# Pair products in quarters of the array, and the last two column tiles in stretches of 304 and 240 tokens, in one layer of a hybrid recurrent decoder

## The chip, the core and the metric

The kernel runs on one core of a Trainium2 chip. A core has a matrix engine (TensorE, here PE; its weight loads are listed apart as PEld), a vector engine (DVE), a scalar engine (ACT), a general engine (POOL), and a queue engine (SP) that issues most of the DMAs. The engines run side by side; each works through its own list of instructions in order and waits on semaphores for the others. The metric is the time of one execution in microseconds (us), lower is better. Before the change the median of three executions is 925.21 us (924.53 to 926.5).

## What is computed

One decoder layer is run for 512 prompt tokens and 8 x 4 sample tokens, which together are the 544 columns of every activation. One input projection feeds three recurrent branches (GLA, mLSTM, HGRN2); their gated sum goes through an output projection and a LayerNorm, then through an MLP and a second LayerNorm. Two of the branches, GLA and HGRN2, are this recurrence, which the kernel evaluates in chunks:

```python
def step(s, blk):
    qc, kc, vc, gc = blk
    b = jnp.cumsum(gc, axis=1)
    o_inter = jnp.einsum("bthk,bhkv->bthv", qc * jnp.exp(b), s)
    rel = jnp.exp(jnp.where(causal, b[:, :, None] - b[:, None, :], -jnp.inf))
    att = jnp.sum(qc[:, :, None] * kc[:, None, :] * rel, axis=-1)
    o_intra = jnp.einsum("btsh,bshv->bthv", att, vc)
...
hid = jnp.square(jax.nn.relu(x @ lp["w_ff_up"]))
x = _layernorm(DN_ALPHA * x + (hid @ lp["w_ff_down"]), lp["ln2_g"], lp["ln2_b"])
```

`att` is a matrix of pair products: entry (t, s), for a query token t and a key token s not after it. The outputs are the layer's result, transposed, and the new recurrent states.

## The kernel before, in words

Activations lie transposed: 128 features on the partitions, 544 tokens along them. A weight matrix comes in tiles of 128 output features (column tiles). For each, `wload` issues a DMA from SP, copies the tile on ACT into a rounded high part `wh` and subtracts on DVE the low part `wl`; `mm` (line 157) then runs three matmuls for each 128 rows of the weight (high x high, high x low, low x high), each on two halves of 272 tokens. These are the matmuls `g` of line 170. `wh` and `wl` have three buffers from the merge stage on, so a tile's copy waits until the PE has finished the tile three loads earlier. The result lies in a pair of PSUM banks, of which there are two pairs.

The two gated recurrences are in `gated` (line 363), first GLA ("gla"), then HGRN2 ("hg"). Tokens come in units u: two of 256 prompt tokens (u = 0, 1), each of C = 2 chunks of R = 128, and the 32 sample tokens (u = 2). `levels(u)` builds the pair products of a unit in a tile `at`: first the diagonal (matmuls `dps`, line 381, then ACT copies of an identity scaled by each head's diagonal, line 388), then the rest by levels m = 64, 32, 16, 8, 4, 2, 1. At a level a block of 2m tokens gives the products of its first m keys with its last m queries. For each level DVE and ACT make the scaled keys `K` (tile ke, line 407) and queries `Q` (tile qe, line 414), the PE multiplies them (`lv`, line 422), and DVE writes the valid entries into `at` under a mask (line 426). Each level's matmul covers all 128 keys of a chunk at once and so also products that no block needs; the mask drops them. ke and qe have two buffers each, used in turn. `chunk(u, c)` then forms the chunk's output `o` from `at` and the state `S` (lines 482, 485), the state update `kvp` (line 490), a norm over each head (`rms_rows`: ACT square, DVE reduce, ACT logarithm and exponential `ss`, DVE product `on`), a transpose `oT` on the PE and its product with the gate. `sample` is the same for u = 2, with matmuls `ox` (line 527) that write 32 PSUM partitions each.

Between these small steps stand background matmuls `g` of column tiles that do not depend on the recurrence. No table sets their order: a scheduler in the framework simulates the program and places each instruction on its engine's list; evacuations and weight copies carry a high priority.

At the end, the last two column tiles of the MLP (features 6 and 7 of 8) are kept back and run by halves of the tokens, so that the second LayerNorm of the first half overlaps the matmuls of the second. `last(i, hf, sl)` runs one tile on one half, `ln_sums` and `ln_end` form mean and inverse deviation (`ne`, `rstd`), and then for each of eight feature tiles DVE adds `ne` (line 1132) and multiplies by `rstd` (line 1136), ACT applies scale and offset (line 1140), and SP stores pairs of tiles (line 1142).

Of the kernel before, what the change touches and what calls it, by code (L numbers as in the profile page):

```python
# [6 lines left out]
F32 = mybir.dt.float32  # L7
# [22 lines left out]
ADDP, MULP, AFFD = (), (), ()  # L30
# [12 lines left out]
def build(tc, I, O):  # L43
    nc = tc.nc
    with ExitStack() as ctx:
# [59 lines left out]
        nc.scalar.dma_start(out=mf_[:, 0:448], in_=I["lmask"])  # L105
        lmask = const.tile([128, 7, 64], I32, name="lmask")
        nc.vector.tensor_copy(lmask.rearrange("p a b -> p (a b)"), mf_[:, 0:448])
        mf2 = wp.tile([128, 1024], F32, tag="raw", name="mf2", bufs=3)
        nc.scalar.dma_start(out=mf2[:, 0:160], in_=I["cmask"])
# [3 lines left out]
        nc.vector.tensor_copy(smask, mf2[:, 128:160])  # L113
        identb = const.tile([128, 128], BF16, name="identb")
# [42 lines left out]
        def mm(ps, units, ah, al, ext=0, halves_=(0, 1), between=None):  # L157


            nk = sum(u[2] for u in units)  # L160
            k = 0
            for u, (h, l, n) in enumerate(units):
                if u and between:
                    between()
                for i in range(n):
                    wh, wl = h[:, i * 128:(i + 1) * 128], l[:, i * 128:(i + 1) * 128]
                    for s, (w, a) in enumerate(((wh, ah), (wh, al), (wl, ah))):
                        for hf in halves_:
                            w_ = HT + (ext if hf else 0)
                            nc.tensor.matmul(  # L170
                                ps[:, hf, 0:w_], w, a(k)[:, hf * HT:hf * HT + w_],
                                start=(k == 0 and s == 0), stop=(k == nk - 1 and s == 2))
                    k += 1
# [189 lines left out]
        def gated(q, k, b, sc, dv, vtok, sname, nt, gate):  # L363
# [5 lines left out]
            def levels(u):  # L369
# [9 lines left out]
                for c in range(C):  # L379
                    for p in range(2):  # L380
                        nc.tensor.matmul(dps[0:R, c * 4 + p * 2:c * 4 + p * 2 + 2], qk[:, p, c * R:(c + 1) * R], headsel,  # L381
                                         start=(c == 0 and p == 0), stop=(c == C - 1 and p == 1))
                dsb = t1.tile([128, 8], F32, tag="dsb", name="dsb")
                nc.vector.tensor_copy(dsb[0:R, 0:4 * C], dps[0:R, 0:4 * C])
                at = kqp.tile([128, 8, 128], F32, tag="at", name="at", bufs=2)
                atv = at[0:R, 0:4 * C, 0:R]
                for j in range(4 * C):
                    nc.scalar.activation(out=at[0:R, j, 0:R], in_=ident[0:R, 0:R], func=AF.Copy, scale=dsb[0:R, j:j + 1])

                for li, m in enumerate(LEVELS):  # L390
                    if 2 * m > B:
                        continue
                    n = L // (2 * m)
                    nr = R // (2 * m)
                    blk = lambda a: a.rearrange("p a (n m) -> p a n m", m=2 * m)
                    K, Q = ke[li % 2], qe[li % 2]
                    bb = blk(bv)
                    ref = bb[:, :, :, m - 1:m].to_broadcast([128, 2, n, m])
                    E = tile2([128, 2, 256], "E")
                    Ev = blk(E[:, :, 0:L])  # L400
                    if m > 1:
                        ref2 = bb[:, :, :, m - 1:m].to_broadcast([128, 2, n, 2 * m])
                        nc.vector.tensor_tensor(out=Ev, in0=bb, in1=ref2, op=ALU.subtract)
                        nc.scalar.activation(out=Ev[:, :, :, 0:m], in_=Ev[:, :, :, 0:m], func=AF.Exp, scale=-sc)
                        nc.scalar.activation(out=Ev[:, :, :, m:2 * m], in_=Ev[:, :, :, m:2 * m], func=AF.Exp, scale=sc)
# [12 lines left out]
                    H = R // 2  # L418
                    for c in range(C):
                        for p in range(2):  # L420
                            o = (c * 2 + p) * 2 * H
                            nc.tensor.matmul(  # L422
                                lv[0:R, o:o + 2 * H].rearrange("p (a b) -> p a b", a=2),
                                Kv[:, p, c * R:(c + 1) * R], Q[:, p, :, c * H:(c + 1) * H],
                                start=(c == 0 and p == 0), stop=(c == C - 1 and p == 1))
                    nc.vector.copy_predicated(
                        atv.rearrange("p h (n m) -> p h n m", m=2 * m)[:, :, :, m:2 * m],
                        lmask[0:R, li, 0:H].rearrange("p (n m) -> p n m", m=m)[:, None].to_broadcast([R, 4 * C, nr, m]),
                        lv[0:R, 0:4 * C * H].rearrange("p (h n m) -> p h n m", h=4 * C, m=m))
                    yield  # L430
                yield
# [412 lines left out]
        def open_kq():  # L844
            st, kqp = pool("kq", 1, "right")
            ke = [kqp.tile([128, 2, 256], F32, name=f"ke{i}") for i in range(2)]
            qe = [kqp.tile([128, 2, 2, 128], F32, name=f"qe{i}") for i in range(2)]
            for t in ke + qe:
                nc.gpsimd.memset(t, 0.0)
            return st, kqp, ke, qe  # L850
# [23 lines left out]
        kqs, kqp, ke, qe = open_kq()  # L874
# [85 lines left out]
        kqs, kqp, ke, qe = open_kq()  # L960
# [52 lines left out]
        def ln_sums(hf, stop=True):  # L1013
            s = slice(hf * HT, (hf + 1) * HT)
            ps = [psr.tile([128, 512], F32, tag="r", name=n) for n in ("m1", "m2")]
            for p, a in zip(ps, (a1, a2)):
                nc.tensor.matmul(p[:, 0:HT], onesn, a[:, s], start=True, stop=stop)  # L1017
            return ps

        def ln_end(hf, sums, more=()):  # L1020
            s = slice(hf * HT, (hf + 1) * HT)
            p1, p2 = sums
            for p, a in zip(sums, more):
                nc.tensor.matmul(p[:, 0:HT], onesn, a, start=False, stop=True)
            e2 = rstd[:, s]
            nc.scalar.activation(out=e2, in_=p1[:, 0:HT], func=AF.Square)
            nc.vector.tensor_tensor(out=e2, in0=p2[:, 0:HT], in1=e2, op=ALU.subtract)
            nc.scalar.activation(out=ne[:, s], in_=p1[:, 0:HT], func=AF.Copy, scale=-1.0)
# [24 lines left out]
        for hf in range(2):  # L1053
            ln_end(hf, ln_sums(hf))
# [55 lines left out]
        def last(i, hf, sl, between=None):  # L1110
            y = x1[:, KD - 2 + i, sl]
            mm(pss[i], units[2 * i:2 * i + 2], hh_, hl_, halves_=(hf,), between=between)
            sq = ftile("sq")
            with tc.high_priority(OFF):
                nc.vector.tensor_tensor(out=y, in0=y, in1=pss[i][:, hf, 0:HT], op=ALU.add)
                nc.scalar.activation(out=sq[:, sl], in_=y, func=AF.Square)
            return y, sq[:, sl]

        for hf in range(2):
            sl = slice(hf * HT, (hf + 1) * HT)  # L1120
# [5 lines left out]
            more = last(1, hf, sl, lambda: ends.append(ln_sums(hf, False)))  # L1126
            with tc.high_priority(OFF):
                ln_end(hf, ends[0], more)
            for m in range(KD):
                y = x1[:, m, sl]  # L1130
                eng = nc.gpsimd if m in ADDP else nc.vector
                eng.tensor_tensor(out=y, in0=y, in1=ne[:, sl], op=ALU.add)
            for m in range(KD):
                y = x1[:, m, sl]
                eng = nc.gpsimd if m in MULP else nc.vector
                eng.tensor_tensor(out=y, in0=y, in1=rstd[:, sl], op=ALU.mult)
                if m in AFFD:
# [14 lines left out]
def _pack(v):  # L1152
# [45 lines left out]
    lmask = np.zeros((128, 7, 64), f)  # L1198
    for i, m in enumerate(LEVELS):
        j = np.arange(64)  # L1200
        lmask[:, i] = ((s[:, None] // (2 * m) == j[None] // m) & (s[:, None] % (2 * m) < m))
# [21 lines left out]
        ident=np.eye(128, dtype=f), lmask=lmask.reshape(128, 448), cmask=np.concatenate([cmask, sm], 1), small=small, lastsel=last,  # L1223
# [42 lines left out]
```

## Time and profile before

| what | value |
|---|---|
| median of three executions | 925.21 us |
| the profiled execution | 923.02 us, of which its span 921.2 us |
| PE busy | 902.4 us |
| DVE busy | 574.3 us |
| ACT busy | 438.3 us |
| POOL busy | 49.6 us |
| GLA recurrence, roughly | 181 to 287 us of the span |
| HGRN2 recurrence, roughly | 312 to 420 us |
| after the last matmul | 911 to 921.2 us |

The span runs from the first to the last recorded instruction. A line such as "L422" is the kernel's line 422. In a timeline a row gives the start, the length of the whole run of like instructions, engine, line, operation, output and inputs, shapes and count; in brackets the engine's idle time before it and what ended it. A float32 matmul of the program shows as two matmuls in the trace, since it is run in two passes; the program's own list, in the section on the change, counts it once.

### The profile page before, as it was taken

To read this page: it belongs to the slowest core of one execution; us is meant where nothing else is said; L and a number is where in the kernel's file an instruction comes from. 1 tells how busy PE (TensorE), PEld (TensorE's weight loads), DVE (VectorE), ACT (ScalarE), POOL (GpSimd) and SP (SyncE) were. 2 spreads that over 40 slices of the span, in tenths; PEclk is the share of its full clock that TensorE was granted. 3 is DMA by queue.
4 is the path that set the end of the run, shared out by engine and by line. 5 is a ranking of instruction groups with operands and counts; after the bars stand their busy time and mean duration, and the time that the engine had idled before them with its cause. 6 is when DMAs were issued, how large, how long until landed. Compare 5 with 4: busy or idle time off the path is not lost.

```text
span 921.2 us, 17477 instructions
## 1 busy us (share of the span) xinstructions
PE 902.4 (98%) x7257; PEld 886.6 (96%) x7257; DVE 574.3 (62%) x1008; ACT 438.3 (48%) x826; POOL 49.6 (5%) x63
## 2 busy tenths in 40 slices
PE   9999999999998999999999999999999999999995
PEld 8998999999998999999999999999999999999994
DVE  5886567788697779785568755554333455444525
ACT  5395323677445875634544455442222345542305
POOL 1301230001001101000000000000000000000000
PEclk9999999999999999999999999999999999999998
DMA  7321242133321113122244222222222222222202
GB/s 267 126 70 69 62 133 83 49 102 89 127 69 41 52 54 98 56 71 86 89 146 142 81 92 92 93 92 75 87 92 92 92 90 74 90 92 92 92 1 98
DMA packets 38335, 82.87 MB, mean 90 GB/s; under 512 B 13156, under 2 KB 19332, under 8 KB 38256
## 3 DMA queue, kind: packets, MB, share of 16 engines
q1 hardware_dynamic: 25664, 73.41, 24.6%
q10 hardware_dynamic: 12528, 8.33, 3.2%
q8 instruction: 57, 0.93, 0.4%
q14 instruction: 22, 0.18, 0.1%
q0 software_dynamic: 64, 0.02, 0.0%
HBM read 76.51 MB, written 5.09 MB: 89 GB/s over the span
## 4 chain that ended last, share of the span: by engine, by line
PE 97%; DVE 2%; ACT 1%; issue 0%; ACTq 0%; DVEq 0%
PE g L170 83%; PE lv L422 3%; PE g L92 3%; PE o L482 1%; PE qkp L701 1%; PE oT L298 0%; PE o L485 0%; PE vt L271 0%; PE kvp L490 0%; PE m L1017 0%; PE na L743 0%; ACT merged L1140 0%; PE wps L64 0%; PE dps L381 0%; PE sp L718 0%; PE kvm L754 0%
## 5 line engine op out<-in xcount | busy, mean ns | idle before, releaser
L154 DVE TENSOR_TENSOR wl<-raw,wh 128x1024 fp32r<-128x1024 f32 (+2 forms) x139 | 154.8, 1113 | 136.9 <-ACT wh L153 136.0
L153 ACT ACTIVATE wh<-raw 128x1024 fp32r<-128x1024 f32 (+2 forms) x139 | 133.3, 959 | 200.9 <-PE g L170 169.3
L170 PE MATMUL g<-xh,wl 128*128 128x272 f32 x752 | 161.1, 291 | 0.0
L170 PE MATMUL g<-xh,wh 128*128 128x272 f32 x752 | 159.8, 291 | 0.3 <-DVE z L863 0.3
L170 PE MATMUL g<-xl,wh 128*128 128x272 f32 x752 | 157.0, 289 | 0.0
L170 PEld LDWEIGHTS g<-xh,wh 128*128 128x128 f32 x752 | 118.7, 189 | 1.8 <-DVE z L863 0.5
L170 PEld LDWEIGHTS g<-xh,wl 128*128 128x128 f32 x752 | 119.0, 188 | 1.1 <-issue 0.2
L170 PEld LDWEIGHTS g<-xl,wh 128*128 128x128 f32 x752 | 118.4, 188 | 0.1
L170 PE MATMUL g<-x1l,wh 128*128 128x272 f32 (+1 forms) x512 | 106.7, 289 | 0.0
L170 PE MATMUL g<-x1h,wh 128*128 128x272 f32 (+1 forms) x512 | 106.4, 289 | 0.0
L170 PE MATMUL g<-x1h,wl 128*128 128x272 f32 (+1 forms) x512 | 106.3, 289 | 0.0
L170 PEld LDWEIGHTS g<-x1l,wh 128*128 128x128 f32 x512 | 81.3, 189 | 0.1
L170 PEld LDWEIGHTS g<-x1h,wh 128*128 128x128 f32 x512 | 81.0, 189 | 0.0
L170 PEld LDWEIGHTS g<-x1h,wl 128*128 128x128 f32 x512 | 80.9, 188 | 0.0
L1070 ACT ACTIVATE relu<-relu,gw 128x544 f32<-128x544 f32 x32 | 24.0, 750 | 78.9 <-DVE relu L1069 78.9
L170 PE MATMUL g<-hidl,wh 128*128 128x272 f32 x280 | 58.2, 289 | 0.0
L170 PE MATMUL g<-hidh,wh 128*128 128x272 f32 x280 | 58.1, 288 | 0.0
L170 PE MATMUL g<-hidh,wl 128*128 128x272 f32 x280 | 58.0, 288 | 0.0
L170 PEld LDWEIGHTS g<-hidl,wh 128*128 128x128 f32 x280 | 44.1, 189 | 0.0
L170 PEld LDWEIGHTS g<-hidh,wh 128*128 128x128 f32 x280 | 44.0, 188 | 0.0
L170 PEld LDWEIGHTS g<-hidh,wl 128*128 128x128 f32 x280 | 44.0, 188 | 0.0
L170 PE MATMUL g<-hdw,wh 128*128 128x272 f32 x168 | 34.8, 289 | 0.0
(399 smaller groups left out, 1633.6 us busy)
## 6 DMA issues: line engine op xcount, KB each, us to landing
raw<-in_wff SPq DMA_DIRECT2D x64, 512.0 KB
raw<-in_win SPq DMA_DIRECT2D x47, 512.0 KB
raw<-in_wout SPq DMA_DIRECT2D x8, 512.0 KB
xr<-in_xT SPq DMA_DIRECT2D x15, 272.0 KB
out_yT<-merged SPq DMA_DIRECT2D x8, 272.0 KB
fw<-in_wfirst ACTq DMA_DIRECT2D x7, 256.0 KB
raw<-in_wup_ml SPq DMA_DIRECT2D x8, 192.0 KB
raw<-in_wup_gla SPq DMA_DIRECT2D x8, 192.0 KB
```

The costliest lines, as they stand in the source:

```text
L92: nc.tensor.matmul(first_ps[i][hf], w[:, i * 128:(i + 1) * 128], a[:, k, hf * HT:(hf + 1) * HT], start=(k == 0 and n == 0), stop=(k == KD ...
L153: nc.scalar.activation(out=h[:, 0:n], in_=raw[:, 0:n], func=AF.Copy)
L154: nc.vector.tensor_tensor(out=l[:, 0:n], in0=raw[:, 0:n], in1=h[:, 0:n].bitcast(F32), op=ALU.subtract)
L170: nc.tensor.matmul(ps[:, hf, 0:w_], w, a(k)[:, hf * HT:hf * HT + w_], start=(k == 0 and s == 0), stop=(k == nk - 1 and s == 2))
L422: nc.tensor.matmul(lv[0:R, o:o + 2 * H].rearrange("p (a b) -> p a b", a=2), Kv[:, p, c * R:(c + 1) * R], Q[:, p, :, c * H:(c + 1) * H], st ...
L482: nc.tensor.matmul(o[:, h * dv:(h + 1) * dv], at[:, c * 4 + h, :], vtok[:, cc, h * dv:(h + 1) * dv], start=(h == 0), stop=(cc == 0 and h = ...
L701: nc.tensor.matmul(ps[0:96, hf, 0:HT], w[:, i, h, :], a[h][:, hf * HT:(hf + 1) * HT], start=(n == 0), stop=(n == 2))
L1070: nc.scalar.activation(out=r_, in_=r_, func=AF.Relu, bias=gw[:, 1:2])
```

## The change

Three things are changed.

Pair products. The level matmuls of the units u = 0 and 1 are cut by keys. For m = 16 and below a matmul takes 32 keys (32 columns of the array) and the 16 queries of each of two heads that belong to them, and there are four of them side by side for each chunk and pair of heads, writing PSUM partitions 0-31, 32-63, 64-95 and 96-127. For m = 32 there are two with 32 keys each, for m = 64 one with 64 keys. The diagonal `dps` is cut in four in the same way. The results of m = 16 and below and the diagonal now go into a small tile `ar` (128 x 8 x 32, the diagonal 32 x 32 blocks); the diagonal is written by one DVE product with a repeated identity `identr`, in place of the ACT copies. m = 64 and m = 32 go straight into `at` by plain copies, the second block of m = 32 on ACT. At the end of a unit four ACT copies put the blocks of `ar` into `at`. `at` is now two fixed tiles `ats`, set to zero on POOL by `open_kq`.

Last column tiles. The halves of 272 and 272 tokens become 304 (`LASTT`) and 240; `mm` takes a list of (bank, first, last) in place of the halves.

Scale and offset. In the second stretch feature tiles 6 and 7 (`AFFD`) get scale and offset on DVE; the other six stay on ACT.

```diff
-ADDP, MULP, AFFD = (), (), ()
+LASTT = 304
+AFFD = (6, 7)
...
-                        for hf in halves_:
-                            w_ = HT + (ext if hf else 0)
+                        for bank, t0, t1_ in parts:
+                            w_ = t1_ - t0 + (ext if bank else 0)
...
-                        nc.tensor.matmul(dps[0:R, c * 4 + p * 2:c * 4 + p * 2 + 2], qk[:, p, c * R:(c + 1) * R], headsel,
-                                         start=(c == 0 and p == 0), stop=(c == C - 1 and p == 1))
-                dsb = t1.tile([128, 8], F32, tag="dsb", name="dsb")
-                nc.vector.tensor_copy(dsb[0:R, 0:4 * C], dps[0:R, 0:4 * C])
-                at = kqp.tile([128, 8, 128], F32, tag="at", name="at", bufs=2)
-                atv = at[0:R, 0:4 * C, 0:R]
-                for j in range(4 * C):
-                    nc.scalar.activation(out=at[0:R, j, 0:R], in_=ident[0:R, 0:R], func=AF.Copy, scale=dsb[0:R, j:j + 1])
+                        for g in range(R // 32):
+                            nc.tensor.matmul(dps[32 * g:32 * g + 32, c * 4 + p * 2:c * 4 + p * 2 + 2],
+                                             qk[:, p, c * R + 32 * g:c * R + 32 * g + 32], headsel,
+                                             start=(c == 0 and p == 0), stop=(c == C - 1 and p == 1))
+                ar = kqp.tile([128, 8, 32], F32, tag="ar", name="ar", bufs=2)
+                arv = ar[0:R, 0:4 * C]
+                nc.vector.tensor_tensor(out=arv, in0=dps[0:R, 0:4 * C, None].to_broadcast([R, 4 * C, 32]),
+                                        in1=identr[0:R, None, :].to_broadcast([R, 4 * C, 32]), op=ALU.mult)
+                at = ats[u] if u < 2 else ar
...
-                            nc.tensor.matmul(
-                                lv[0:R, o:o + 2 * H].rearrange("p (a b) -> p a b", a=2),
-                                Kv[:, p, c * R:(c + 1) * R], Q[:, p, :, c * H:(c + 1) * H],
-                                start=(c == 0 and p == 0), stop=(c == C - 1 and p == 1))
-                    nc.vector.copy_predicated(
-                        atv.rearrange("p h (n m) -> p h n m", m=2 * m)[:, :, :, m:2 * m],
-                        lmask[0:R, li, 0:H].rearrange("p (n m) -> p n m", m=m)[:, None].to_broadcast([R, 4 * C, nr, m]),
-                        lv[0:R, 0:4 * C * H].rearrange("p (h n m) -> p h n m", h=4 * C, m=m))
+                    w = max(m, 16)
+                    M = max(m, 32)
+                    step = max(2 * m, 32)
...
+                            for g in range(R // step):
+                                k0 = g * step
+                                nc.tensor.matmul(
+                                    lv[k0:k0 + M, (c * 2 + p) * 2 * w:(c * 2 + p + 1) * 2 * w].rearrange("p (a b) -> p a b", a=2),
+                                    Kv[:, p, c * R + k0:c * R + k0 + M], Q[:, p, :, (c * R + k0) // 2:(c * R + k0) // 2 + w],
+                                    start=(c == 0 and p == 0), stop=(c == C - 1 and p == 1))
+                    if m > 16:
+                        for g in range(R // step):
+                            k0 = g * step
+                            src = lv[k0:k0 + M, 0:8 * w].rearrange("p (h q) -> p h q", h=8)
+                            dst = at[k0:k0 + M, :, k0 + m:k0 + 2 * m]
+                            if g:
+                                nc.scalar.activation(out=dst, in_=src, func=AF.Copy)
+                            else:
+                                nc.vector.tensor_copy(dst, src)
+                    else:
+                        nb = 16 // m
+                        nc.vector.copy_predicated(
+                            arv.rearrange("p h (n m) -> p h n m", m=2 * m)[:, :, :, m:2 * m],
+                            lmask[0:R, li, :].rearrange("p (n m) -> p n m", m=m)[:, None].to_broadcast([R, 4 * C, nb, m]),
+                            lv[0:R, 0:4 * C * 16].rearrange("p (h n m) -> p h n m", h=4 * C, m=m))
...
+                if u < 2:
+                    for g in range(4):
+                        gs = slice(32 * g, 32 * g + 32)
+                        nc.scalar.activation(out=at[gs, :, gs], in_=ar[gs], func=AF.Copy)
...
-            for t in ke + qe:
+            ats = [kqp.tile([128, 8, 128], F32, name=f"at{i}") for i in range(2)]
+            for t in ke + qe + ats:
                 nc.gpsimd.memset(t, 0.0)
...
-        for hf in range(2):
-            sl = slice(hf * HT, (hf + 1) * HT)
+        for hf, sl in enumerate((slice(0, LASTT), slice(LASTT, T))):
...
-                if m in AFFD:
+                if hf and m in AFFD:
                     nc.vector.tensor_scalar(y, y, vcol(V_L2G + m), vcol(V_L2B + m), ALU.mult, ALU.add)
```

The scheduler also places instructions anew in the two recurrences. Three places matter below.

The first is the end of the GLA recurrence on the PE: the last level of unit 1, and the first chunk's output up to its transpose. Before:

```order
L422 MATMUL lv<-qe_2114,kg 128x128 x4
L444 MATMUL ktp<-ident,W 128x128 x4
L170 MATMUL g<-xh,wh 128x272
L170 MATMUL g<-xl,wh 128x272 x2
L170 MATMUL g<-xh,wl 128x272 x2
L482 MATMUL o<-gvt,at 128x96 x2
L490 MATMUL kvp<-gvt,kt 64x96 x4
L485 MATMUL o<-S,Qt 128x192
L482 MATMUL o<-gvt,at 128x96 x2
L485 MATMUL o<-S,Qt 128x192
L298 MATMUL oT<-ident,on 128x128 x3
```

Now, from the first chunk's last product with S on (31 background matmuls have been put between `ktp` and the first `o`, 5 stood there before):

```order
L509 MATMUL o<-S,Qt 128x192
L514 MATMUL kvp<-gvt,kt 64x96 x4
L173 MATMUL g<-xh,wh 128x272
L173 MATMUL g<-xl,wh 128x272 x2
L173 MATMUL g<-xh,wl 128x272 x2
L173 MATMUL g<-xh,wh 128x272 x2
L173 MATMUL g<-xl,wh 128x272 x2
L173 MATMUL g<-xh,wl 128x272 x2
L173 MATMUL g<-xh,wh 128x272 x2
L173 MATMUL g<-xl,wh 128x272 x2
L173 MATMUL g<-xh,wl 128x272 x2
L301 MATMUL oT<-ident,on 128x128 x3
```

So 17 background matmuls, the last of their column tile, now stand between the output and its transpose. On ACT at the same place, from the copies of unit 1 to the second chunk's square, before:

```order
L448 ACTIVATE kt<-ktp 128x512
L153 ACTIVATE wh<-raw 128x1024
L306 ACTIVATE sq<-o 128x384
L309 ACTIVATE ss<-ss,epsn 128x4
L310 ACTIVATE ss<-ss 128x4
L306 ACTIVATE sq<-o 128x384
```

and now:

```order
L454 ACTIVATE at_2119<-ar 32x8x32 x4
L472 ACTIVATE kt<-ktp 128x512
L309 ACTIVATE sq<-o 128x384
L312 ACTIVATE ss<-ss,epsn 128x4
L156 ACTIVATE wh<-raw 128x1024
L313 ACTIVATE ss<-ss 128x4
L309 ACTIVATE sq<-o 128x384
```

The weight copy `wh`, which stood ahead of the square, now stands between the logarithm and the exponential of the norm; its buffer is the one that the 17 matmuls above read.

The second place is the end of the HGRN2 recurrence on DVE: the last chunk's norm, its product with the gate, and the evacuation `gb` of a merge gate. Before:

```order
L308 TENSOR_REDUCE ss<-sq 128x4
L312 TENSOR_TENSOR on<-o,ss 128x256
L227 TENSOR_SCALAR gb<-g,vec 128x544
L300 TENSOR_TENSOR hgate<-oT,hgate 128x2x128
L154 TENSOR_TENSOR wl<-raw,wh 128x256
L192 TENSOR_TENSOR hl<-hgate,hh 128x544 x2
```

and now:

```order
L315 TENSOR_TENSOR on<-o,ss 128x256
L303 TENSOR_TENSOR hgate<-oT,hgate 128x2x128
L230 TENSOR_SCALAR gb<-g,vec 128x544
L157 TENSOR_TENSOR wl<-raw,wh 128x256
L195 TENSOR_TENSOR hl<-hgate,hh 128x544 x2
```

The product with the gate now comes ahead of the evacuation; on the PE six background matmuls stand behind that transpose, where none stood before, and the evacuation waits for them.

The third place is unit 0 of the GLA recurrence on the PE, from the last background matmuls ahead of the levels m = 32 and 16 to the next ones; `ox` are the sample tokens' products with the states and `kvs` their state updates. Before:

```order
L170 MATMUL g<-xl,wh 128x272 x2
L422 MATMUL lv<-qe_2115,ke_2113 128x128 x4
L527 MATMUL ox<-Ss,qx 32x96 x8
L422 MATMUL lv<-qe_2114,ke_2112 128x128 x4
L534 MATMUL kvs<-vx,k_2169 128x384
L527 MATMUL ox<-Ss,qx 32x96 x8
L170 MATMUL g<-xh,wl 128x272 x2
```

and now:

```order
L173 MATMUL g<-hh,wl 128x272 x2
L431 MATMUL lv<-qe_2117,ke_2115 32x64 x8
L551 MATMUL ox<-Ss,qx 32x96 x8
L431 MATMUL lv<-qe_2116,ke_2114 32x32 x16
L558 MATMUL kvs<-vx,k_2170 128x384
L551 MATMUL ox<-Ss,qx 32x96 x8
L173 MATMUL g<-hh,wh 128x272 x2
```

The order of the groups is the same, but each level is now 8 or 16 products on 32 partitions where it was 4 on 128, the kind that `ox` already was; so three neighbouring groups on the PE are of one kind. HGRN2's unit 0 has the same pattern.

At the end of the program the DVE's list has two more instructions, `merged<-merged,vec` on 128 x 240, behind the last product with `rstd`, and ACT's last run of scale and offset falls from eight to six.

More of the change, by code (lines that the diff above doesn't have):

```diff
@@ L155, in wload, with mm @@
             return h, l
-        def mm(ps, units, ah, al, ext=0, halves_=(0, 1), between=None):
+        def mm(ps, units, ah, al, ext=0, parts=((0, 0, HT), (1, HT, T)), between=None):
             nk = sum(u[2] for u in units)
@@ L959, in build @@
         hgate = feed_gate(M_HT, 2, V_HG, "hgate", True, rest)
-        kqs, kqp, ke, qe = open_kq()
+        kqs, kqp, ke, qe, ats = open_kq()
         gated(qh, kh, bh, 1.0, 64, hvt, "hg", 2, hgate)
@@ L1011, in ln_tile, with ln_sums, ln_end @@
                 nc.vector.tensor_tensor(out=a2[:, sl], in0=a2[:, sl], in1=sq[:, sl], op=ALU.add)
-        def ln_sums(hf, stop=True):
-            s = slice(hf * HT, (hf + 1) * HT)
+        def ln_sums(s, stop=True):
             ps = [psr.tile([128, 512], F32, tag="r", name=n) for n in ("m1", "m2")]
+            ps = [p[:, 0:s.stop - s.start] for p in ps]
             for p, a in zip(ps, (a1, a2)):
-                nc.tensor.matmul(p[:, 0:HT], onesn, a[:, s], start=True, stop=stop)
+                nc.tensor.matmul(p, onesn, a[:, s], start=True, stop=stop)
             return ps
-        def ln_end(hf, sums, more=()):
-            s = slice(hf * HT, (hf + 1) * HT)
+        def ln_end(s, sums, more=()):
             p1, p2 = sums
             for p, a in zip(sums, more):
-                nc.tensor.matmul(p[:, 0:HT], onesn, a, start=False, stop=True)
+                nc.tensor.matmul(p, onesn, a, start=False, stop=True)
             e2 = rstd[:, s]
-            nc.scalar.activation(out=e2, in_=p1[:, 0:HT], func=AF.Square)
-            nc.vector.tensor_tensor(out=e2, in0=p2[:, 0:HT], in1=e2, op=ALU.subtract)
-            nc.scalar.activation(out=ne[:, s], in_=p1[:, 0:HT], func=AF.Copy, scale=-1.0)
+            nc.scalar.activation(out=e2, in_=p1, func=AF.Square)
+            nc.vector.tensor_tensor(out=e2, in0=p2, in1=e2, op=ALU.subtract)
+            nc.scalar.activation(out=ne[:, s], in_=p1, func=AF.Copy, scale=-1.0)
             nc.scalar.activation(out=e2, in_=e2, func=AF.Ln, bias=epsl)
@@ L1052, in build @@
             ln_tile(x1, m, slice(0, T), put_x1)
-        for hf in range(2):
-            ln_end(hf, ln_sums(hf))
+        for s in (slice(0, HT), slice(HT, T)):
+            ln_end(s, ln_sums(s))
         mps.close()
@@ L1111, in last @@
             y = x1[:, KD - 2 + i, sl]
-            mm(pss[i], units[2 * i:2 * i + 2], hh_, hl_, halves_=(hf,), between=between)
+            mm(pss[i], units[2 * i:2 * i + 2], hh_, hl_, parts=((hf, sl.start, sl.stop),), between=between)
             sq = ftile("sq")
             with tc.high_priority(OFF):
-                nc.vector.tensor_tensor(out=y, in0=y, in1=pss[i][:, hf, 0:HT], op=ALU.add)
+                nc.vector.tensor_tensor(out=y, in0=y, in1=pss[i][:, hf, 0:sl.stop - sl.start], op=ALU.add)
                 nc.scalar.activation(out=sq[:, sl], in_=y, func=AF.Square)
             return y, sq[:, sl]
-        for hf in range(2):
-            sl = slice(hf * HT, (hf + 1) * HT)
+        for hf, sl in enumerate((slice(0, LASTT), slice(LASTT, T))):
             y, sq = last(0, hf, sl)
@@ L1222, in _pack @@
         wfirst=win[0:NF].reshape(NF, 128, 8, 128).transpose(2, 1, 0, 3).reshape(8, 128, NF * 128), vec=vec, gatew=gw, wqk=wqk, sel=sel,
-        ident=np.eye(128, dtype=f), lmask=lmask.reshape(128, 448), cmask=np.concatenate([cmask, sm], 1), small=small, lastsel=last,
+        ident=np.eye(128, dtype=f), lmask=lmask.reshape(128, 112), cmask=np.concatenate([cmask, sm, r == np.arange(32)[None]], 1), small=small, lastsel=last,
         gla=gla.reshape(2, 128, 8, 96), hg=hg.reshape(2, 128, 8, 64), mC=mC,
```

35 lines of the change are left out of this document (16 added, 19 removed).

## The prediction

> **What bounds the kernel now.** I read the page's first rows, then the busy time by stretches.
>
> ```profile
> span 921.2 us, 17477 instructions
> PE 902.4 (98%) x7257; PEld 886.6 (96%) x7257; DVE 574.3 (62%) x1008; ACT 438.3 (48%) x826; POOL 49.6 (5%) x63
> PE g L170 83%; PE lv L422 3%; PE g L92 3%; PE o L482 1%; PE qkp L701 1%; PE oT L298 0%; PE o L485 0%; PE vt L271 0%; PE kvp L490 0%; PE m L1017 0%; PE na L743 0%; ACT merged L1140 0%; PE wps L64 0%; PE dps L381 0%; PE sp L718 0%; PE kvm L754 0%
> ```
>
> The chain of work that ended last (third row) is PE from start to end, with ACT's last scale and offset behind it. The level products `lv` are 3% of it, the largest share after the background matmuls `g`.
>
> ```profile
> 181.00:287.00 106.00, 102.99 (x852) 99.46 (x850) 84.40 (x159) 62.41 (x147) 6.97 (x9) 0.98 0.28 91
> 312.00:420.00 108.00, 106.46 (x910) 104.20 (x909) 87.03 (x173) 64.15 (x150) 4.13 (x3) 1.00 0.22 68
> 911.00:921.20 10.20, 0.00 (x0) 0.00 (x0) 5.26 (x15) 4.77 (x10) 0.00 (x0) 0.69 0.31 109
> ```
>
> These are GLA, HGRN2 and the end (after the bounds and length: busy time of PE, PEld, DVE, ACT and POOL with counts, PE's granted clock, DMA). In the recurrences PE rests 3.0 and 1.5 us, most of it in two waits:
>
> ```profile
> PE oT L298 <- DVE on L312: 2.6, 1, 2.6
> PE g L170 <- ACT hh L191: 1.9, 1, 1.9
> ```
>
> So there is little idle time to win inside the recurrences. What can be won is PE work in the levels, up to 4.5 us of waits, and some of the 10.2 us in which PE has nothing left.
>
> **The cost of a small group on PE.** The trace shows what `ox` (32 columns of the array, four column groups in turn) costs between two groups of `lv`:
>
> ```profile
> 202.01 0.41 PE L170 MATMUL g<-xh,wh 128*128 128x272 f32 x2
> ...
> 202.26 0.41 PE L170 MATMUL g<-xl,wh 128*128 128x272 f32 x2
> ...
> 202.51 1.05 PE L422 MATMUL lv<-qe,ke 128*128 128x128 f32 x8
> ...
> 203.50 0.54 PE L527 MATMUL ox<-Ss,qx 128*32 128x96 f32 x16
> ...
> 203.97 1.16 PE L422 MATMUL lv<-qe,ke 128*128 128x128 f32 x8
> ...
> L422 PE MATMUL lv<-qe,ke x200: 196/275/377, 181.5 to 396.1; 128*128 128x128 f32 x96, 128*32 128x32 f32 x4
> ...
> L527 PE MATMUL ox<-Ss,qx x64: 217/244/270, 203.5 to 330.8; 128*32 128x96 f32 x32, 128*32 128x64 f32 x32
> ...
> 330.63 0.42 PE L527 MATMUL ox<-Ss,qx 128*32 128x64 f32 x14
> ```
>
> One `lv` lasts 0.275 (median), so eight start (1.05 - 0.275) / 7 = 0.111 apart: a level of today costs 8 x 0.111 = 0.89 us. The last of the first eight starts at 202.51 + 7 x 0.111 = 203.28. The second eight run 1.16, 0.11 more than seven even steps make, so their second starts 203.97 + 1.16 - 0.275 - 6 x 0.111 = 204.19. From 203.28 to 204.19 are 0.91 us, of which two steps of `lv` are 0.22. The `ox` starts are (0.54 - 0.244) / 15 = 0.020 apart, four to a round of 0.08; four rounds are 0.32. What is left, 0.91 - 0.22 - 0.32 = **0.37**, is the price of going to the narrow form and back; I take 0.35. With 64 columns of data instead of 96 the steps shrink to (0.42 - 0.217) / 13 = 0.0156, a round to 0.062.
>
> **Levels m = 16 and below** (five levels in four units: 20 groups). Now 16 program products, 32 in the trace, eight rounds of four. Their data is 32 columns wide, a form with two rows nearby in which products follow each other in one column group:
>
> ```profile
> 181.49 0.31 PE L422 MATMUL lv<-qe,ke 128*32 128x32 f32 x4
> ...
> 319.55 0.63 PE L513 MATMUL ol<-hvt,at 32*32 32x64 f32 x8
> ```
>
> The first gives (0.31 - 0.196) / 3 = 0.038 a step, and the step bounds a round where four groups run beside each other. On the second, 0.63 for eight products of 64 columns is about 0.06 a step, as a round of `ox` with 64. I take 0.04 a round: 0.35 + 8 x 0.04 = 0.67, which is 0.22 less than 0.89; 20 groups give **-4.4**. Bounds: a round that shrinks with the data, 0.111 x 32 / 128 = 0.028 (group 0.57, -6.4), or that stays as long as the 96-column one, 0.08 (0.99, +2.0).
>
> **The diagonal** (four groups) runs today as
>
> ```profile
> 183.66 0.95 PE L381 MATMUL dps<-small,qk 128*128 128x2 f32 x8
> ```
>
> less the last one's 0.25, 0.10 a step, 0.80 in all; now 0.67: **-0.5**. **m = 32** has 16 products of 64 columns in two column groups. At `ox`'s 0.0156 a product it is 0.35 + 0.25 = 0.60, at the `ol` row's 0.06 a pair 0.35 + 0.48 = 0.83; I take 0.83: **-0.2** for four (bounds -1.2, +0.7 if nothing is shared). **m = 64** keeps its eight products at 0.111 but now with half of the array: if that form too pays the change, 0.35 each, **+1.4**; if not, 0.
>
> **Neighbours.** Where a narrow group stands beside `ox` or another narrow group, one change is saved: in each unit 0 twice (the third place of the order), and m = 8 to 4 and 4 to 2 in HGRN2 once each, six times; a `kvs` splits a group twice. Net -4 x 0.35 = **-1.4**. The array comes to -4.4 - 0.5 - 0.2 + 1.4 - 1.4 = **-5.1**.
>
> [...]
>
> **DVE, ACT and POOL in the recurrences.**
>
> ```profile
> L426 DVE COPY_PREDICATED at<-lmask,lv 128x512 f32<-128x512 int32 x28 | 25.0, 893 | 10.3 <-PE lv L422 9.1 <-ACT at L388 1.0
> L388 ACT ACTIVATE at<-ident,dsb 128x128 f32<-128x128 f32 x32 | 10.0, 388 | 1.3 <-DVE dsb L384 1.3
> L405 ACT ACTIVATE E<-E 128x256 f32<-128x256 f32 x24 | 9.6, 415 | 0.3
> ```
>
> Masked copies of 512 columns at 0.89 become 20 of 128 columns (a quarter, at least 0.25) and a few plain copies; DVE loses some 15 us of work. ACT loses 10.0 and gets 20 copies near the third row's 0.415, 8.3. DVE already waits 9.1 us for the PE's levels, so none of this is on the path. Four ACT copies of `ar`, 1.7 us, now stand between a unit's last level and `o`. In GLA's unit 1 they lie beside the 31 background matmuls, 31 x 0.125 = 3.9 us (in the rows at 202.01 and 202.26 two take 0.25); elsewhere the cover is thinner, and each level's copy is a new link to the next. I put **+0.5** (0 to +7: if none of the four units had cover, 4 x 1.7).
>
> ```profile
> 84.10 0.99 POOL L849 MEMSET qe<- 128x512 f32 x2
> 85.05 0.40 POOL L723 TENSOR_TENSOR rd<-rrs,small 36x128 fp32r<-36x128 f32 x1
> ...
> 91.77 0.24 PE L725 MATMUL dp<-rd,ones 36*32 36x128 f32 x1
> ...
> POOL qk L377 <- DVE qh L955: 8.9, 1, 8.9
> ```
>
> Setting `ats` to zero adds four times twice `qe`'s 0.50, 4.0 us on POOL. The first two stand ahead of `rd`, whose reader starts 6.3 us later; the others in POOL's wait of 8.9: **0**. Without that cover 2 us each.
>
> **The end of GLA.** `wh` has moved behind the output's square, and 17 matmuls (2.1 us) stand between output and transpose.
>
> ```profile
> 277.35 1.05 ACT L153 ACTIVATE wh<-raw 128x1024 fp32r<-128x1024 f32 x1
> 278.43 1.22 DVE L154 TENSOR_TENSOR wl<-raw,wh 128x1024 fp32r<-128x1024 f32 x1 [0.17 <-ACT wh L153]
> ...
> 282.14 0.56 DVE L312 TENSOR_TENSOR on<-o,ss 128x384 f32<-128x384 f32 x1 [0.60 <-ACT ss L310]
> ```
>
> But `wh` overwrites the buffer that these 17 read, so it starts when they end, and the exponential and `on` come behind it on their engines: 1.05 + up to 1.22 + 0.56 = 2.8 before the transpose, against 2.6 today. After today's wait the clock falls:
>
> ```profile
> 283.20:286.80 3.60, 3.60 (x22) 3.15 (x20) 1.94 (x3) 0.46 (x1) 0.99 (x2) 0.53 0.02 5
> ```
>
> 3.6 us at 0.53 cost some 1.6, which should stay. **0** (-4.2 if wait and slow stretch both go, +0.5).
>
> **The end of HGRN2.**
>
> ```profile
> 418.03 0.42 ACT L153 ACTIVATE wh<-raw 128x256 fp32r<-128x256 f32 x1 [2.59 <-PE g L170]
> 418.28 0.78 DVE L227 TENSOR_SCALAR gb<-g,vec 128x544 f32<-128x544 f32 x1 [2.39 <-PE g L170]
> 418.99 0.42 DVE L300 TENSOR_TENSOR hgate<-oT,hgate 128x256 f32<-128x256 f32 x1
> 419.10 0.66 ACT L218 ACTIVATE gb<-gb 128x544 f32<-128x544 f32 x1 [0.66 <-DVE gb L227]
> 419.66 1.19 ACT L191 ACTIVATE hh<-hgate 128x544 fp32r<-128x544 f32 x2
> ```
>
> The product `hgate` loses the 0.78 of `gb` ahead of it, and six matmuls (0.75) cover the rest; the 0.42 of `wh` may come between. The wait falls from 1.9 by 0.75 + 0.78 - 0.42 = 1.1 at most; I take **-0.8** (0 to -1.5).
>
> **The end of the program.**
>
> ```profile
> 908.77 0.43 ACT L1116 ACTIVATE sq<-merged 128x272 f32<-128x272 f32 x1 [1.05 <-DVE merged L1115]
> ...
> 913.37 2.89 DVE L1136 TENSOR_TENSOR merged<-merged,rstd 128x272 f32<-128x272 f32 x8
> 913.84 4.14 ACT L1140 ACTIVATE merged<-merged,vec 128x272 f32<-128x272 f32 x8 [2.18 <-DVE merged L1136]
> ...
> L1142 SPq DMA_DIRECT2D out_yT<-merged x8: 372/373/410, 904.4 to 918.0; - x8
> ```
>
> PE's sum over 544 tokens stays. DVE's 16 passes of 272 take 0.361 each; with 240, some 0.03 less, 0.25 over the eight `ne` sums that ACT waits for. ACT then runs 6 x 0.49 (a little under 4.14 / 8 = 0.52) = 2.9 instead of 4.14, while DVE's two extra ones end about together with it: **-1.5** in all. The last two DMA issues then stand closer, 0.37 each: +0.4; and the first stretch's ACT work, 304 wide, runs some 1.4 later, past the 1.05 in which ACT rested ahead of `sq`: +0.3. Net **-0.8** (-2 to +0.5).
>
> **Sum.** -5.1 + 0.5 + 0 + 0 - 0.8 - 0.8 = **-6.2 us**. The execution of the trace took 923.02, its span 921.2; it becomes 916.8. The median of the runs, 925.21, lies 2.2 above that one; the same difference gives **919.0**.
>
> **The rivals.** A measurement of this kernel tells about 0.2%, 1.85 us, from no change: "faster" is below 923.4, "slower" above 927.1.
> - *No gain in the array.* Each product takes 18 ns to start, between `ox`'s 15.6 and 20, whatever its data: a group is 0.35 + 32 x 0.018 = 0.93, 20 groups give +0.8 instead of -4.4, total -1.0: 924.2. For it: no row has four column groups with only 32 columns; against it, the step fell by a fifth from 96 to 64 columns. 0.11, all in "same".
> - *Slower: the quarters do not run beside each other.* All 32 products follow at the 0.038 of the 181.49 row: 0.35 + 32 x 0.038 = 1.57 a group, 20 x 0.68 = +13.6 where I put -4.4, total +11.8: about 937. A group loses from a step of (0.89 - 0.35) / 32 = 17 ns on, the whole is over +1.85 from 0.18 a group or 23 ns on. `ox` speaks against it, since its four groups do run together; but they read 64 and 96 columns, and a floor per product would show only in shorter ones. 0.11. [...]
> - *New waits eat it.* With a stretch of the 1.7 us of `ar` copies open in two or three units, +3 to +5: 922 to 924. DVE's and ACT's lighter load speaks against it. 0.11, of which 0.07 within 0.2%.
> - *Better.* GLA's wait and its slow clock both go, or rounds take 0.028: -10 to -12, 913 to 915. 0.07. Against it, `wh`'s buffer.
> - *The forecast*, 915 to 922: 0.60.
>
> Faster 0.60 + 0.07 + 0.04 = 0.71, same 0.11 + 0.07 = 0.18, slower 0.11. The range from 912.5 to 925 leaves out the slower case and a little beside it.
>
> **What would show it.** Right: a group of m = 16 or less takes about 0.3 us from first to last start, with some 0.2 before and 0.17 behind; the wait of `oT` at GLA's end is still near 3 us with a slow stretch behind it; the wait for `hh` is near 1; from the last matmul to the span's end are 0.8 us less; masked copies are under half of 25.0 us. Wrong: starts 30 to 40 ns apart in a group, new rows of PE waiting for DVE or ACT around `lv` and `o`, or `oT` without a wait.

## The result and the profile after

The changed kernel takes 912.35 us (median of four executions, 910.82 to 914.86), the kernel before in the same session 925.86 us. The ratio is 0.9858 with a 95% interval of 0.9829 to 0.9886, a gain of 10.6 to 15.8 us. The forecast was 919.0 in a range of 912.5 to 925.0: faster was right, the size about half of what came; the time lies 0.15 us below the range's lower end, well inside the measurement's own interval.

The page of the profile after, its first rows:

```profile
span 909.4 us, 18677 instructions
PE 890.6 (98%) x7865; PEld 869.5 (96%) x7865; DVE 564.4 (62%) x1011; ACT 434.5 (48%) x804; POOL 54.2 (6%) x67
```

PE is still the bound; it has 608 matmuls more and is busy 11.8 us less. The stretches that answer to those shown before (GLA, HGRN2, and the end from the last matmul on):

```profile
181.00:287.00 106.00, 102.27 (x1198) 96.13 (x1197) 83.32 (x168) 65.86 (x146) 9.49 (x11) 1.00 0.30 92
302.00:410.00 108.00, 107.18 (x1260) 102.50 (x1258) 84.54 (x177) 67.26 (x154) 4.21 (x3) 1.00 0.23 70
899.10:909.40 10.30, 0.33 (x2) 0.00 (x0) 6.13 (x19) 4.08 (x9) 0.00 (x0) 0.71 0.38 128
```

In the view of PE's waits, the long ones of the recurrences are these (the first row answers to 2.6 before, the second is new and lies in GLA, the third answers to 1.9):

```profile
PE oT L301 <- DVE on L315: 2.9, 1, 2.9
...
PE g L173 <- DVE gb L230: 0.8, 1, 0.8
PE g L173 <- ACT hh L194: 0.8, 1, 0.8
```

What a level costs can be read directly from PE's timeline, where a group stands alone between background matmuls. Before, m = 2 of GLA's unit 1:

```profile
270.15 0.41 PE L170 MATMUL g<-xh,wl 128*128 128x272 f32 x2
270.40 1.05 PE L422 MATMUL lv<-qe,ke 128*128 128x128 f32 x8
271.21 0.49 PE L170 MATMUL g<-xh,wh 128*128 128x272 f32 x2
271.55 0.41 PE L170 MATMUL g<-xl,wh 128*128 128x272 f32 x2
```

and after, a level of the same unit:

```profile
262.87 0.41 PE L173 MATMUL g<-xl,wh 128*128 128x272 f32 x2
263.21 0.46 PE L431 MATMUL lv<-qe,ke 128*32 128x32 f32 x32
263.60 0.52 PE L173 MATMUL g<-xh,wl 128*128 128x272 f32 x2
263.96 0.41 PE L173 MATMUL g<-xh,wh 128*128 128x272 f32 x2
```

From the first row's start to the last one's are 1.40 and 1.09 us, with four background matmuls of 0.125 each in either. The group itself costs 0.90 before and **0.59** after. Its 32 products start within 0.46 - 0.196 = 0.26 us (0.196 is the median of one by the group's source view), 8.5 ns apart; the other 0.33 is the change of form, of which 0.09 falls ahead of the first product (0.34 from 262.87 instead of 0.25) and the rest behind the last.

### The profile page after: what moved, and what is told of

Same layout as the page of the kernel before. It is cut to its first block, busy times and chain, and to the rows that moved or that the text cites. A ratio compares the mean times of both kernels' runs of the same rounds, so it can differ in the third digit from the quotient of the medians.

```text
span 909.4 us, 18677 instructions
## 1 busy us (share of the span) xinstructions
PE 890.6 (98%) x7865; PEld 869.5 (96%) x7865; DVE 564.4 (62%) x1011; ACT 434.5 (48%) x804; POOL 54.2 (6%) x67
## 4 chain that ended last, share of the span: by engine, by line
PE 95%; DVE 2%; ACT 1%; DMA 1%; issue 0%; ACTq 0%
PE g L173 84%; PE g L93 2%; PE lv L431 2%; PE o L506 1%; ACT merged L1161 1%; PE qkp L725 1%; DVE merged L1154 1%; PE oT L301 1%; DMA fw<-in_wfirst 1%; PE vt L274 0%; PE o L509 0%; PE na L767 0%; PE kvp L514 0%; PE sp L742 0%; PE kvs L558 0%; PE m L1042 0%
## 5 line engine op out<-in xcount | busy, mean ns | idle before, releaser
L173 PE MATMUL g<-xh,wh 128*128 128x272 f32 x752 | 161.9, 293 | 0.3 <-DVE z L888 0.3
L173 PE MATMUL g<-xh,wl 128*128 128x272 f32 x752 | 158.3, 290 | 0.0
```

The source lines that it names most:

```text
L173: nc.tensor.matmul(ps[:, bank, 0:w_], w, a(k)[:, t0:t0 + w_], start=(k == 0 and s == 0), stop=(k == nk - 1 and s == 2))
```

## The experiments

All times are medians beside the kernel before on the same chip, unless only one execution is named. A ratio with its interval is the recorded one, which need not equal the quotient of the two medians; a gain with an interval is worked out from the ratio.

**The pair products alone.** The last column tiles go back to 272 and 272 tokens:

```diff
-LASTT = 304
-AFFD = (6, 7)
+LASTT = 272
+AFFD = ()
```

> The new pair products with the last column tiles as before (272 and 272 tokens, all scale and offset on ACT). My theory: the level groups and the diagonal give about -9.0 us (from the two traces: 20 groups of m=16 and below at -0.305, 4 diagonals at -0.337, the rest from m=32 and neighbours), the end of HGRN2 -1.2, the end of GLA 0 to -1.9 according to whether the clock falls there; so -10.0 to -12.0 us against before, ratio 0.987 to 0.989. Rival, that the last column tiles bring a large share (3 us or more): -7 to -9 us, ratio 0.990 to 0.992.

Measured: 914.39 against 924.27 us, ratio 0.9888 (0.987 to 0.9906), -10.4 us (-9.9 by the medians), as expected. The pair products and the order that comes with them are most of the gain. The number is more likely too small than too large: the six executions have mean granted clocks of 0.991 to 0.996, and the profiled one lost some 3.4 us ((1 - 0.57) x 8, an estimate from its clock of 0.57 from 280 to 288 us) to the slow stretch that the next experiment is about.

**The last column tiles alone.** The kernel before, with `mm` by parts, `LASTT = 304`, `AFFD = (6, 7)` and the functions of the tail as in the diff, and nothing of the recurrences.

> The kernel before with the stretches of 304 and 240 tokens and scale and offset of the last two feature tiles on DVE, pair products as before. My theory: -1.2 us (from the last matmul's start to the span's end 11.5 before and 10.3 after), bounds -0.5 to -2; ratio 0.998 to 0.9995. Rival: -3 us or more, ratio below 0.997. In the trace the end from the last matmul's start is 10.3 +- 0.3, and the clock falls after the wait of oT at the end of GLA as in the trace of before, if that belongs to the order there; if it comes and goes by itself, it may be absent.

Measured: 923.53 against 924.27 us, ratio 0.9988 (0.9976 to 1.0001). By the ratio that is -1.1 us with an interval from -2.2 to +0.1 (-0.7 by the medians), where the forecast had -0.8; the rival's 3 us are excluded. Its trace also answers the question on the clock. The order at the end of GLA is that of before, PE waits for `on` 2.6 us as before, and yet the clock stays up behind the wait. These are 6 us behind it, first of the kernel before, then of this one (the column ahead of the last two is the granted clock):

```profile
283.00:289.00 6.00, 6.00 (x39) 5.43 (x39) 3.76 (x9) 2.38 (x4) 0.99 (x2) 0.72 0.01 3
```

```profile
283.00:289.00 6.00, 4.04 (x35) 3.73 (x36) 4.44 (x11) 2.32 (x6) 0.99 (x2) 1.00 0.21 83
```

(This execution reached GLA some 2 us later, so the second stretch still holds the end of the wait.) The slow stretch is therefore no property of that order.

**The quarters one after the other.** The same products, in another order:

```diff
-                    for c in range(C):
-                        for p in range(2):
-                            for g in range(R // step):
+                    for g in range(R // step):
+                        for c in range(C):
+                            for p in range(2):
```

> The changed kernel with the products of a level issued one quarter of the array after the other (eight in a row in the same 32 columns) instead of the four quarters in turn. My theory, that the four run beside each other and one quarter alone takes 0.038 us a product: a group of m=16 and below takes 31 x 0.038 = 1.2 us from first to last start instead of 0.26, so 20 x 0.9 = +18, and m=32 about +2: some +20 us against the changed kernel, about 930. Rival, that a product of 32 columns is simply short and the PE takes the next one whatever its columns: groups stay at 0.26, the time at about 911.

Measured: 921.29 us in one execution. The timeline of a level of GLA's unit 1:

```profile
265.96 0.41 PE L173 MATMUL g<-xl,wh 128*128 128x272 f32 x2
266.31 0.90 PE L431 MATMUL lv<-qe,ke 128*32 128x32 f32 x32
267.14 0.52 PE L173 MATMUL g<-xh,wl 128*128 128x272 f32 x2
267.49 0.41 PE L173 MATMUL g<-xh,wh 128*128 128x272 f32 x2
```

The 32 starts take 0.90 - 0.196 = 0.70 us instead of 0.26, 22.7 ns apart. So the four quarters do run beside each other, by a factor of 2.7, and the rival is excluded. The expected 0.038 us a product within one quarter was too much; it came from a row of only four. 20 groups by 0.44 are 8.8 us, and the one execution is 8.9 above the 912.35 of the changed kernel: the time follows the groups one for one, where some +20 us had been expected. (The edit also reorders m = 32, which costs 0.25 more in each unit 1, and groups beside other narrow products lose less than 0.44. Cut out of both timelines one by one, all groups together lose 8.9.)

**Every small product twice.** In units 0 and 1, for m = 16 and below, all products are issued again into columns 256 and up of the same bank, which nothing reads:

```diff
+                    nd = 2 if m <= 16 and u < 2 else 1
+                    for d in range(nd):
...
+                                    o = 256 * d + (c * 2 + p) * 2 * w
```

> The changed kernel with every product of the levels m=16 and below issued a second time in units 0 and 1, into columns of the same bank that nothing reads. My theory: only the body of a group doubles, 64 starts in 0.53 us instead of 32 in 0.26, the step stays 8.4 ns, entry 0.09, exit 0.13 and the late second background matmul 0.11 stay; 20 x 0.27 = +5.4 us. Rival, that the price is per group and products inside it are free: 0 to +1. Rival, that a deeper run is bound by issue at 15 ns or more: +9 or more.

Measured: 915.42 us in one execution. A group of HGRN2:

```profile
331.45 0.41 PE L173 MATMUL g<-xh,wl 128*128 128x272 f32 x2
331.79 0.76 PE L434 MATMUL lv<-qe,ke 128*32 128x32 f32 x64
332.48 0.52 PE L173 MATMUL g<-xh,wh 128*128 128x272 f32 x2
332.83 0.41 PE L173 MATMUL g<-xl,wh 128*128 128x272 f32 x2
```

64 starts take 0.56 us, 9 ns apart, and the group costs 1.38 - 0.50 = 0.88: 0.29 more for 32 more products, the change of form once. 20 groups would be +5.8. This excludes both rivals: products in a longer run are neither free nor do they take 15 ns. The time rose by only about 3, because the schedule came out otherwise: `oT` at GLA's end does not wait its 2.9 any more, while PE waits 1.4 for `merged` and rests 0.9 inside a group of HGRN2, both new. The step is shown by the rows; the total does not show it.

**m = 64 on the whole array.**

```diff
+                                W_ = R if m == 64 else M
...
-                                    lv[k0:k0 + M, (c * 2 + p) * 2 * w:(c * 2 + p + 1) * 2 * w].rearrange("p (a b) -> p a b", a=2),
-                                    Kv[:, p, c * R + k0:c * R + k0 + M], Q[:, p, :, (c * R + k0) // 2:(c * R + k0) // 2 + w],
+                                    lv[k0:k0 + W_, (c * 2 + p) * 2 * w:(c * 2 + p + 1) * 2 * w].rearrange("p (a b) -> p a b", a=2),
+                                    Kv[:, p, c * R + k0:c * R + k0 + W_], Q[:, p, :, (c * R + k0) // 2:(c * R + k0) // 2 + w],
```

> The changed kernel with m=64 issued on all 128 keys again (half of them products that nothing reads), its plain copy unchanged. My theory, that half of the array is as much a change of form as a quarter: the last units' groups lose 0.3 each, those of the first units, which stand beside the sample tokens' narrow products, 0.0 to 0.1; -0.6 to -0.9 us against the changed kernel. Rival, that 64 columns pay no change: 0.

Measured: 913.95 us, against 913.19 of the changed kernel beside it. The medians say nothing here: single executions lie 1 to 2 us apart, and the profile of this one has one of the two longest slow stretches (within 278 to 288 us, below). The traces do tell. In GLA's unit 1 the group stands between a background matmul and the first `o`. Of the changed kernel:

```profile
233.25 0.29 PE L173 MATMUL g<-hh,wl 128*128 128x272 f32 x1
233.47 1.09 PE L431 MATMUL lv<-qe,ke 128*64 128x128 f32 x8
...
235.55 0.55 PE L514 MATMUL kvp<-gvt,kt 128*64 128x96 f32 x8
```

and of this experiment:

```profile
233.49 0.29 PE L173 MATMUL g<-hh,wl 128*128 128x272 f32 x1
233.62 1.05 PE L432 MATMUL lv<-qe,ke 128*128 128x128 f32 x8
...
235.46 0.55 PE L515 MATMUL kvp<-gvt,kt 128*64 128x96 f32 x8
```

From `g` to `kvp` 2.30 and 1.97 us: half of the array pays 0.33, the same change as a quarter, as expected. HGRN2's unit 1 gives the same; beside the narrow products of unit 0 it is 0.12 in GLA and -0.06 in HGRN2. Together the cut of m = 64 costs 0.33 + 0.32 + 0.12 - 0.06 = 0.7 us.

**The changed kernel once more.**

> The changed kernel once more, for a narrower interval and a second profile. My theory, that the stretch at half clock behind the wait of oT at the end of GLA comes and goes by itself in both kernels (absent in the profile of the change, present in one of the new pair products with the same wait of 2.9): the ratio stays at 0.986 to 0.989, the wait stays at 2.9, and single executions lie apart by 2 to 4 us with the granted clock going along. Rival, that the change removes it: all executions near 0.997 of full clock.

Measured: 913.19 against 924.81 us, ratio 0.9864 (0.9845 to 0.9884). Its four executions, with the clock averaged over the whole run: 912.07 at 0.997, 912.89 and 913.49 at 0.995, 914.26 at 0.993. So the time goes with the clock here too, and the rival falls: the profile of this one has the same wait of 2.9 as the first profile of the change, and a slow stretch behind it that the first did not have. The stretch in three profiles with that order, the first profile of the change:

```profile
280.00:288.00 8.00, 7.96 (x66) 7.64 (x67) 7.03 (x12) 3.57 (x7) 2.27 (x3) 1.00 0.24 79
```

this one, of the same program:

```profile
280.00:286.00 6.00, 5.24 (x32) 4.61 (x33) 3.55 (x9) 1.59 (x3) 1.85 (x2) 0.72 0.24 87
```

and m = 64 on the whole array:

```profile
278.00:288.00 10.00, 8.03 (x43) 7.40 (x44) 6.77 (x12) 3.19 (x6) 1.85 (x2) 0.66 0.16 52
```

**The norm ahead of the weight copy.** In `chunk`, the norm of the output gets the priority of the weight copies; the scheduler then puts the exponential and `on` ahead of `wh` and `wl` at GLA's end:

```diff
-                on = rms_rows(128, o[:, 0:d4].rearrange("p (a b) -> p a b", a=4), dv)
+                with tc.high_priority(OFF):
+                    on = rms_rows(128, o[:, 0:d4].rearrange("p (a b) -> p a b", a=4), dv)
```

> The changed kernel with the norm of a chunk's output at the priority of the weight copies, so that at the end of GLA the exponential and the product on stand ahead of the next weight copy wh and wl on ACT and DVE. My theory, that wh and wl (1.04 and 1.22) are what the transpose waits for: the wait of oT falls from 2.9 to 0.8 +- 0.4, and the stretch at half clock behind it goes in all executions, since PE does not rest long enough; -2 us, and another -0.5 to -1 in the median; ratio to before 0.983 to 0.986. Rival, that the wait is only moved, to the matmuls that need wh and wl: 0, with a new wait of g for wl or wh.

Measured: 909.36 us, ratio 0.9819 (0.9801 to 0.9838), 3.8 below the changed kernel beside it. In the timeline of PE, ACT and DVE hardly a gap is left in the chain from the norm's exponential to the transpose:

```profile
277.80 0.21 ACT L313 ACTIVATE ss<-ss 128x4 f32<-128x4 f32 x1
...
278.04 0.56 DVE L315 TENSOR_TENSOR on<-o,ss 128x384 f32<-128x384 f32 x1 [0.25 <-ACT ss L313]
...
278.29 1.06 ACT L156 ACTIVATE wh<-raw 128x1024 fp32r<-128x1024 f32 x1 [0.29 <-PE g L173]
278.74 0.52 PE L301 MATMUL oT<-ident,on 128*128 128x128 f32 x3 [0.23 <-DVE on L315]
```

`oT` waits 0.23 instead of 2.92; the copy comes behind, and in time: of the waits that PE has for `wl` or `wh`, the longest is 0.6, and it stood in other profiles of the changed pair products too. Of the 3.8, 2.7 are the wait, which fell further than to the expected 0.8. The edit acts on every chunk, so there is more in it: in this profile PE does not wait for `hh` at HGRN2's end (0.8 in the changed kernel), and it waits 0.5 for `qh` and 0.4 for `ar`, which it did not; these three nearly cancel. The rest, about 1, fits an estimate of what the slow stretch cost on average (0 and 1.7 us in the two profiles of the changed kernel), but was not measured by itself. All five executions have a mean clock of 0.995 to 0.997. That the slow stretch is gone in all of them is not shown, since 0.995 is also the mean clock of the repeated run's profile, which has one.

**Both edits.**

> Both of the last two edits. My theory: they add, -3 to -4 us against the changed kernel, ratio to before 0.982 to 0.985. Rival: as e7 alone or no better than the changed kernel.

Measured: 907.8 us (907.76 to 908.03, clock 0.996 in all four), ratio 0.9807 (0.9789 to 0.9825): 1.6 below the norm alone, 5.4 below the changed kernel. It beats both kernels. Of the 1.6, 0.7 is the m = 64 step. The rest is not resolved: a wait for `xh` at the start, 1.7 in the profile of the norm alone, is missing in this one, and the intervals are wider than the difference.

## Why the prediction was right in sign and half in size

The two profiles shown at first are not like for like: that of before has a slow stretch at GLA's end, worth 6 x 0.28 = 1.7 us, and that of the change has none. The experiment with the last column tiles alone has the recurrences of before at full clock, so the change is set against that. The views by source line give first and last start of the diagonal's products and of `oT`; first for that experiment, then for the changed kernel:

```profile
L382 PE MATMUL dps<-small,qk x40: 165/251/251, 183.0 to 358.0; 128*128 128x2 f32 x32, 128*32 128x2 f32 x8
...
L299 PE MATMUL oT<-ident,on x25: 221/273/300, 229.7 to 418.7; 128*128 128x128 f32 x20, 32*128 32x32 f32 x5
```

```profile
L385 PE MATMUL dps<-small,qk x136: 171/171/192, 181.8 to 348.2; 128*32 128x2 f32 x136
...
L301 PE MATMUL oT<-ident,on x25: 221/272/329, 224.6 to 408.1; 128*128 128x128 f32 x20, 32*128 32x32 f32 x5
```

235.7 and 226.3 us, -9.4. Six background matmuls (0.75) stood ahead of the last `oT` and stand behind it now, so the gain is 8.7; and PE waits about 0.9 for `gb` where it did not. At GLA's end the two chunks with their wait take 8.1 and 7.9 us of PE beside the background matmuls, which is 0.25 of the gain (both at full clock). The groups' own gain is 8.7 + 0.9 - 0.25: **about 9.4**; cut out of the two timelines one by one, as in the level above, the groups with their neighbours come to 8.9. The prediction had 5.1. This is the step that was mis-sized.

- **Levels m = 16 and below, -4.4 predicted, -6.2 measured** (20 x 0.31). The mechanism was right: a fixed change of form of about 0.35 (measured 0.33) and products side by side. The round of four was put at 0.04 from a row of four products in one quarter; it is 0.034, and with the smaller change the group is 0.59 instead of 0.67. What stood behind that round was wrong too: "the step bounds a round where four groups run beside each other" took a four-product row for a rate, 0.038; a longer run in one quarter goes at 0.023, so that row gave no bound for a round.
- **The diagonal, -0.5 predicted, -1.3 measured.** From PE's timeline of GLA's unit 1, taken as for the levels: before 0.89 (from 232.91 to 234.30 less four background matmuls), after 0.57 (from 228.92 to 229.99 less the same). Before, the prediction counted only the eight starts and not what lies before the next matmul; after, the round was too long.
- **m = 32, -0.2 predicted, -0.7 measured**, 0.17 a group in both units 1. That is a group of 0.72, midway between the two readings of 0.60 and 0.83. **m = 64, +1.4 predicted, +0.7 measured**: right where it stands alone (0.33 against 0.35), nearly free beside narrow products (0.12 and -0.06).
- **Neighbours, -1.4 predicted, about -1.4 measured.** What is left of the groups cut out one by one is 8.9 - 6.2 - 1.3 - 0.7 + 0.7 = 1.4. Most of it lies beside `ox`, as predicted. These are GLA's unit 0, first with the last column tiles alone, then the changed kernel:

```profile
204.38 0.41 PE L171 MATMUL g<-xl,wh 128*128 128x272 f32 x2
204.62 1.05 PE L423 MATMUL lv<-qe,ke 128*128 128x128 f32 x8
...
208.42 0.41 PE L171 MATMUL g<-xl,wh 128*128 128x272 f32 x2
```

```profile
197.92 0.41 PE L173 MATMUL g<-hh,wl 128*128 128x272 f32 x2
198.26 0.58 PE L431 MATMUL lv<-qe,ke 128*32 128x64 f32 x13
...
200.92 0.28 PE L173 MATMUL g<-hh,wl 128*128 128x272 f32 x1
```

From `g` to `g`, less six background matmuls in either, are 3.29 and 2.25 us. Of the difference of 1.04, one group of m = 32 and one of m = 16 explain 0.17 + 0.31; the other 0.56 is what the neighbours save. HGRN2 has 3.22 and 2.09 there, 0.65 saved. The 0.5 between 8.9 and 9.4 lies outside the groups and stays open.

- **New waits, +0.5 predicted**: one of 0.8 to 0.9, for `gb`, not for the levels. PE does not wait for `at` or `ar` in the profile after; the masked copies fell from 25.0 us to 7.1, and ACT's copies of `ar` stayed hidden, as the rows say (of the costliest groups: busy time and mean ns of one, then the engine's idle time before them and what ended it).

```profile
L446 DVE COPY_PREDICATED ar<-lmask,lv 128x128 f32<-128x128 int32 x20 | 7.1, 354 | 6.3 <-PE lv L431 6.2
...
L454 ACT ACTIVATE at<-ar 32x256 f32<-32x256 f32 x16 | 6.6, 414 | 1.1 <-DVE ar L446 0.8
```

- **GLA's end, 0 predicted.** The wait was put at 2.8 and is 2.9, by the chain that was named (the norm experiment shows it: with the copies out of the way it is 0.2). The assumption that failed is that the slow stretch "should stay": it comes and goes, in the changed kernel from run to run, and with the order of before between the kernel before and the last column tiles alone.
- **HGRN2's end, -0.8 predicted.** The wait for `hh` went from 1.9 to 0.8, as the bound of 1.1 allowed.
- **The end, -0.8 predicted**, -1.1 (-2.2 to +0.1) measured alone.

By these terms the change is worth -9.4 - 0.25 + 0.9 - 1.1 - 1.1 = -11 us, against -13.5 and -11.6 by the medians of the two comparisons (-13.1 and -12.6 by the ratios), both with intervals that hold 11. The two profiles' difference, 921.2 - 909.4 = 11.8, has 1.7 of the slow stretch in it for the change, and 1.0 against it, since the first diagonal product starts at 181.8 instead of 180.8: PE waited 1.4 for `xh` at the start, behind a DMA that both kernels issue alike (`fw`, for which ACT waited 3.4 there and 2.5 before).

The time came out nearest to the rival "Better" (913 to 915), but not by what it named: the wait of `oT` is still there, and a round takes 0.034, not 0.028. Of the other rivals, "no gain in the array" and "quarters do not run beside each other" are excluded by the rows and by the quarter-after-quarter run.

## What to carry to other kernels

In this kernel small products that fill a part of the array paid once for the change of form on each visit (0.33 us) and little for each product where neighbours in the order went to different quarters (8.5 to 9 ns, against 22.7 one behind the other in one quarter); so cut where the group is long (0.90 before, 0.59 after), leave a half-array cut whole where it stands alone (0.33 lost, no product saved), and put narrow groups beside each other (0.56 and 0.65 saved beside `ox`). Before crediting a change with a stretch at full clock, look at several profiles of the same program (of two of the changed kernel, one has the slow stretch). A wait for a short chain behind a long weight copy is worth a priority: here the edit brought 3.8 us, 2.7 of them that wait, where the pair products brought 10.

## What the runs showed that was not expected

The slow stretches came in two lengths. The rows above give, as an estimate from the granted clock, (1 - 0.72) x 6 = 1.7 us lost in the kernel before and in the repeated run, which at a clock of 0.50 (that of the windows wholly inside: 284 to 286 us in the kernel before, 282 to 284 in the repeated run) is a stretch of 3.4 us; and (1 - 0.66) x 10 = 3.4 lost with m = 64 whole, where the clock is 0.50 from 280 to 286 us, a stretch of 6.8, twice as long. The pair products alone had such a long one too, 0.66 from 280 to 290 us. The stretch followed a wait of `oT` of 2.6 to 2.9 us, in four of the seven profiles that have this wait; of the three profiles in which `oT` does not wait longer than about 0.2 (both with the norm first, and every product twice) none has it. What sets the two lengths was not shown, and which executions fall into it could not be told ahead.
